# A decoder trunk on one core: retention heads projected with 512 moving columns, reciprocal roots as powers on GpSimd, a shorter last stage

## The chip, the cores and the metric

The kernel runs on one core of a Trainium2 chip. The metric is the device time of one launch in microseconds (us). The engines are named as in the profile: PE is TensorE's matmul side and PEld its weight loads, DVE is VectorE, ACT is ScalarE, POOL is GpSimd, SP is SyncE, which issues most of the DMAs.

## The reference

A residual stream x of 1024 tokens by 1024 channels goes through two layers and a final RMS norm. All is float32. A layer, cut to what matters here:

```python
mod = c_act @ w_ada[layer] + b_ada[layer]
shift, scale, gate = jnp.split(mod[:, None, :], 3, axis=-1)
h = rmsnorm(x, norm_g[layer]) * (1.0 + scale) + shift
proj = jnp.einsum('bld,de->ble', h, w_in[layer])      # one input projection, split into four branches
y_a = hgrn2_branch(...)       # 4 heads, vector decay
y_b = retention_branch(rq, rk, rv, rg, ret_onorm_g[layer])
y_c = ssd_branch(...)         # selective state space, 2 groups
y_d = gla_branch(...)         # 4 heads, vector decay
y = jnp.concatenate([y_a, y_b, y_c, y_d], axis=-1)
x = x + gate * jnp.einsum('ble,ed->bld', y, w_out[layer])
```

The retention branch has four heads of 128 channels: query and key are rotated by position (`[t1*cos - t2*sin, t1*sin + t2*cos]`, halves of 64), a chunked scalar-decay attention follows, then a group RMS norm per head and a SiLU gate. At the end comes `rmsnorm(x, final_g)`.

## The kernel before

**Arithmetic.** The input projection and the output projection are made from operands split in two parts of a rounded float32 type (`fp32r`). A weight tile `raw` is loaded (two buffers), ACT rounds it to `whi` (L408), DVE forms the rest `wlo` (L409), with four buffers for each. The normed input, feature-major, exists as `hh` and `hl` for all tokens. A product is three matmuls: hh*whi, hh*wlo, hl*whi.

**Projections.** There are two forms. `proj_f` (L423 to L425) makes 128 features by 512 tokens, with the weights stationary and 512 moving columns. `proj_t` (L470, L472, L473) makes a unit of 256 features token-major: for each k of eight, and each of eight token tiles, the input tile is stationary and 256 weight columns move. Its eight results lie two to a PSUM bank, four banks of the `pp` tag, all in use until the unit ends. Its weights come as four raw tiles, each with two k. A retention head has two such units: query with key (`rqk`), then value with gate (`rvg`).

**Retention.** `ret_qk` evacuates query and key by a copy on ACT (L842), four multiplications of 128x128 on DVE for each of query and key (L846 to L849), and two sums on POOL (L850, L851), for two token tiles at a time. `vg_proj` evacuates the value on DVE (L740) and the gate with SiLU on ACT (L741). `ret_mix` transposes query and key (L862), makes the scores (L875, L877) and calls `scan` (L664 to L680), which calls the head norm (L544, L548) and brings the result feature-major (L527, L535, L536) for the output projection.

**Roots.** `rsqrt_of` computes (s*scale + eps)^-0.5 on DVE from a bit trick and three Newton steps: L266, L271, L272, then three times L275, L276, L277, twelve tiny instructions one after another. It serves the norm of the input, every head norm, the state-space norm and the final norm.

**Order.** The order of TensorE's instructions is written out by hand. A mixer is a generator that yields how many ns its next product has to wait for others; the function `fill` then takes that much work from the deque `ready`, which holds projections and output projections. `drain` runs `ready` until a given unit has ended. A wrong estimate makes TensorE wait, since its queue is in order. Output projections (`add_out`) take two feature tiles at a time: weights loaded, multiplied by the gate on POOL (L1113), split, then 16 units of six matmuls (L1124) and an addition onto x on DVE (L1129). A unit yields after every third matmul.

In a layer the mixers come in this order: the four hgrn heads, the four gla heads, the two state-space groups, the four retention heads. Retention head 0 is projected while the second state-space group runs (its lines here are L1067, L1085, L1103), head h+1 while head h is mixed. The output projection of the last two feature tiles (6, 7) goes by token tiles, and each tile is normed as it is done: `next_norm` in the first layer, `final_after` in the second.

**The final norm.** For token tiles 0 to 6: squares on ACT (L355), a root on DVE, the tile times the gain on POOL (L1164, 128x1024), the scale on ACT (L1165), the DMA (L1168). The last tile goes in halves: two sums of squares (L1175), a root, two DVE instructions (L1185), two DMAs (L1186).

**The start.** x is loaded, its squares summed on ACT (L355), two roots for four token tiles each, the scaling (L373), transposes (L383). The shift and scale of the first layer are sums over `w_ada` on DVE (L302, L304), whose results `gs` (L320) allow the first `hh` (L400) and the first projections (L423).

Of the kernel before, what the change touches and what calls it, by code (L numbers as in the profile page):

```python
# [11 lines left out]
F32 = mybir.dt.float32  # L12
# [9 lines left out]
P = 128  # L22
# [11 lines left out]
# Columns of the combined input projection.  # L34
# [6 lines left out]
# Feature-major units (128 columns) and token-major units (256 columns).  # L41
# [33 lines left out]
# Per-partition columns, packed: name -> (offset, width).  # L75
# [20 lines left out]
# Rows that are broadcast over partitions.  # L96
# [16 lines left out]
# Constants that depend on shapes alone.  # L113
# [53 lines left out]
def hybrid_trunk(ctx, nc, tc, t_in, out, gamma_c):  # L167
# [94 lines left out]

    def rsqrt_of(ss, n, scale, eps):
        """(ss * scale + eps) ** -0.5, elementwise on [128, n]."""
        t = sm_t("rt", n, w=8)
        vec.tensor_scalar(t, ss, scale, eps, MUL, ADD)  # L266
        return rsqrt(t, n)

    def rsqrt(t, n):
        y = sm_t("ry", n, w=8)  # L270
        vec.tensor_scalar(y.bitcast(I32), t.bitcast(I32), 1, None, ALU.arith_shift_right)  # L271
        vec.tensor_scalar(y.bitcast(I32), y.bitcast(I32), -1, RSQRT_SEED, MUL, ADD)  # L272
        w = sm_t("rw", n, w=8)
        for _ in range(3):
            vec.tensor_tensor(w, y, y, MUL)  # L275
            vec.scalar_tensor_tensor(w, w, -0.5, t, MUL, MUL)  # L276
            vec.scalar_tensor_tensor(y, w, 1.5, y, ADD, MUL)  # L277
        return y
# [10 lines left out]
    def ada_sum(l, c0, n, out_):  # L289
        """Sum over k-tiles of w_ada[k, c0 : c0 + n] * silu(c)[k], per partition."""  # L290
# [32 lines left out]
    def set_gate(l, acc):  # L323
        """The gate on every partition."""
# [9 lines left out]
    # Lower bounds of the forget gates (the first layer's is zero).  # L334
# [28 lines left out]
    def over_rms(ms, ss, engs=(gp,)):  # L363
        """Token tiles over their rms; the last one is where the gate comes later."""
# [11 lines left out]
    def columns(xr):  # L376
        """Tiles xr of 512 tokens, feature-major, for each k."""
# [11 lines left out]
    def modulated(l, half, xr=None, xT=None):  # L389
        """The modulated norm of 512 tokens, feature-major, as the parts hh, hl; a step for each k."""  # L390
# [36 lines left out]
    def proj_f(l, name, evac):  # L427
        """Feature-major: evac(half, ps) takes 512 tokens of a unit's 128 features."""
# [27 lines left out]
    def proj_t(l, name, evac):  # L456
        """Token-major: evac(j, ps) takes token tiles 2j and 2j+1 as ps[128, 2, 256]."""
# [19 lines left out]

    def proj_t_wide(l, name, evac, extra):
# [982 lines left out]
```

## Time and profile before

| | |
|---|---|
| median of 3 runs | 2113.49 us (2113.32 to 2113.72) |
| span of the profiled execution | 2112.7 us |
| PE busy | 2047.3 us, 97% |
| DVE busy | 1318.1 us, 62% |
| ACT busy | 732.0 us, 35% |
| POOL busy | 389.0 us, 18% |
| mean granted TensorE clock | 0.991 |

The profile gives one time for its own execution, the span from the first instruction to the last. The median of the timed runs lies 0.8 us above it. In a row of a timeline stand the start, the duration, the engine, the line, the operation, output and inputs with their shapes, and in brackets how long the engine had been idle and what released it. In a group row stand the count, the busy time, the mean in ns and the idle time before. Durations of matmuls overlap: what a matmul costs is the distance between two starts.

### The profile page before, as it was taken

Reading aid. Unit: us, or ns where it says so; the run is one execution under the profiler, and the core shown is the slowest. Engines: PE = TensorE matmul, PEld = TensorE weight load, DVE = VectorE, ACT = ScalarE, POOL = GpSimd, SP = SyncE. Lnnn points to the kernel's source line nnn. Section 1 sums busy time; section 2 is a strip of 40 time slices with the busy share of each in tenths; the row PEclk is TensorE's granted clock in tenths of the full one; section 3 lists DMA queues with packets and bytes.
Section 4 is the critical chain, followed back from the end, with each engine's and each line's share of the span. In section 5 each row is a group of like instructions: output and inputs, shape, how many; then the busy total and the mean of one; then the engine's idle time right before and its main releaser. Section 6 shows DMA issues by size and latency. Waiting matters only on the chain.

```text
span 2112.7 us, 43480 instructions
## 1 busy us (share of the span) xinstructions
PE 2047.3 (97%) x18052; PEld 1835.8 (87%) x18052; DVE 1318.1 (62%) x3206; ACT 732.0 (35%) x1642; POOL 389.0 (18%) x493
## 2 busy tenths in 40 slices
PE   4999999999999999999999999999999999999996
PEld 3898888899888899999878888878988889999994
DVE  7657845847638576555676574575665676755568
ACT  6432224432333422222263232344233352222223
POOL 3100000000035253112120010000101535401133
PEclk8999999999999999999999999999999999999998
DMA  8233321110111111111122111111111111111111
GB/s 278 83 106 100 94 74 36 32 41 32 41 40 36 41 45 31 51 36 40 37 63 87 56 37 41 36 37 36 37 37 43 36 36 48 39 39 37 41 51 80
DMA packets 67542, 115.75 MB, mean 55 GB/s; under 512 B 9584, under 2 KB 19984, under 8 KB 67344
## 3 DMA queue, kind: packets, MB, share of 16 engines
q1 hardware_dynamic: 67056, 112.24, 16.5%
q8 instruction: 142, 2.33, 0.4%
q10 hardware_dynamic: 288, 0.73, 0.1%
q14 instruction: 56, 0.46, 0.1%
HBM read 108.75 MB, written 4.19 MB: 53 GB/s over the span
## 4 chain that ended last, share of the span: by engine, by line
PE 83%; DVE 11%; ACT 4%; issue 1%; DMA 1%; SPq 0%; DVEq 0%; ACTq 0%
PE pp L1124 14%; PE pp L470 11%; PE pp L472 11%; PE pp L473 11%; PE pp L423 6%; PE pp L425 6%; PE pp L424 6%; PE ms L670 2%; PE sc L587 1%; PE sc L527 1%; DVE b L615 1%; DVE xs L1129 1%; PE po L664 1%; PE sc L664 1%; PE sc L674 1%
## 5 line engine op out<-in xcount | busy, mean ns | idle before, releaser
L470 PE MATMUL pp<-whi,hh 128*128 128x256 f32 x2176 | 628.9, 289 | 0.7 <-ACT b L953 0.7
L472 PE MATMUL pp<-wlo,hh 128*128 128x256 f32 x2176 | 611.5, 281 | 0.0
L473 PE MATMUL pp<-whi,hl 128*128 128x256 f32 x2176 | 611.1, 281 | 0.0
L470 PEld LDWEIGHTS pp<-whi,hh 128*128 128x128 f32 x2176 | 410.3, 189 | 4.4 <-ACT b L953 1.6
L472 PEld LDWEIGHTS pp<-wlo,hh 128*128 128x128 f32 x2176 | 410.5, 189 | 0.8
L473 PEld LDWEIGHTS pp<-whi,hl 128*128 128x128 f32 x2176 | 410.1, 188 | 0.0
L408 ACT CAST whi<-raw 128x512 fp32r<-128x512 f32 x280 | 174.0, 625 | 600.5 <-PE pp L473 302.1
L409 DVE TENSOR_TENSOR wlo<-raw,whi 128x512 fp32r<-128x512 f32 x276 | 207.9, 755 | 250.2 <-ACT whi L408 243.2
L1113 POOL TENSOR_TENSOR raw<-raw,gate_b 128x512 f32<-128x512 f32 x64 | 82.8, 1295 | 1146.4 <-DMA raw<-in_w_out 895.3
L423 PE MATMUL pp<-hh,whi 128*128 128x512 f32 x640 | 272.1, 425 | 12.0 <-ACT hh L400 11.3
L425 PE MATMUL pp<-hl,whi 128*128 128x512 f32 x640 | 254.6, 398 | 1.3 <-DVE hl L401 1.3
L424 PE MATMUL pp<-hh,wlo 128*128 128x512 f32 x640 | 253.7, 396 | 0.0
L1129 DVE TENSOR_TENSOR xs<-xs,pp 128x512 f32<-128x512 f32 x256 | 173.7, 683 | 53.3 <-PE pp L1124 50.9
L1124 PE MATMUL pp<-whi,yh 128*128 128x512 f32 x448 | 189.0, 422 | 0.0
L1124 PE MATMUL pp<-whi,yl 128*128 128x512 f32 x448 | 175.4, 392 | 0.0
L1124 PE MATMUL pp<-wlo,yh 128*128 128x512 f32 x448 | 175.4, 392 | 0.0
L423 PEld LDWEIGHTS pp<-hh,whi 128*128 128x128 f32 x640 | 121.5, 190 | 36.5 <-ACT hh L400 12.6
L425 PEld LDWEIGHTS pp<-hl,whi 128*128 128x128 f32 x640 | 120.8, 189 | 33.2 <-DVE hl L401 4.4
L424 PEld LDWEIGHTS pp<-hh,wlo 128*128 128x128 f32 x640 | 121.6, 190 | 20.9 <-DVE wlo L409 0.2
L1124 PEld LDWEIGHTS pp<-whi,yh 128*128 128x128 f32 x448 | 84.4, 188 | 20.5 <-issue 3.0
L304 DVE SCALAR_TENSOR_TENSOR b<-wa,c_act,b 128x512 f32<-128x512 f32 x84 | 70.2, 835 | 51.2 <-DMA wa<-in_w_ada 50.3
L1124 PEld LDWEIGHTS pp<-whi,yl 128*128 128x128 f32 x448 | 84.1, 188 | 18.8
(242 smaller groups left out, 3195.5 us busy)
## 6 DMA issues: line engine op xcount, KB each, us to landing
raw<-in_wt SPq DMA_DIRECT2D x136, 256.0 KB, 3.0
wa<-in_w_ada SPq DMA_DIRECT2D x96, 256.0 KB, 2.8
raw<-in_wf SPq DMA_DIRECT2D x80, 256.0 KB, 2.6
raw<-in_w_out SPq DMA_DIRECT2D x64, 256.0 KB, 2.5
xs<-in_x SPq DMA_DIRECT2D x8, 512.0 KB, 7.4
out<-b SPq DMA_DIRECT2D x7, 512.0 KB, 2.6
b<-in_wt SPq DMA_DIRECT2D x4, 384.0 KB, 4.8
b<-in_rows SPq DMA_DIRECT2D x4, 256.0 KB, 3.9
```

Source lines behind the costliest of these rows:

```text
L304: vec.scalar_tensor_tensor(acc, w, c_act[:, k : k + 1], acc, MUL, ADD)
L408: act.copy(hi, raw)
L409: eng.tensor_tensor(lo, raw, hi.bitcast(F32), SUB)
L423: pe.matmul(ps, hi[:, j : j + P], hh[half][:, k, :], start=(k == 0), stop=False)
L424: pe.matmul(ps, lo[:, j : j + P], hh[half][:, k, :], start=False, stop=False)
L425: pe.matmul(ps, hi[:, j : j + P], hl[half][:, k, :], start=False, stop=(k == KT - 1))
L470: pe.matmul(o, hhi, hi[:, j : j + 256], start=(k == 0 and m % 2 == 0), stop=False, skip_group_check=True)
L472: pe.matmul(o, hhi, lo[:, j : j + 256], start=False, stop=False, skip_group_check=True)
L473: pe.matmul(o, hlo, hi[:, j : j + 256], start=False, stop=(k == KT - 1), skip_group_check=True)
L1113: gp.tensor_tensor(raw, raw, gate_b[:, nh * 512 : (nh + 1) * 512], MUL)
L1124: pe.matmul(ps, a[:, o : o + P], b, start=(n == 0), stop=(n == 3 * len(kts) - 1))
L1129: vec.tensor_tensor(xv, xv, ps, ADD)
```

## The change

1. **Projection.** A new function `proj_pair` projects the query, key, value and gate of a retention head together, 512 columns. It goes through the tokens in two halves of four tiles; in each half through eight k. For each half and k it loads a raw tile of 512 columns by two DMAs of 128x256, so each weight is loaded and split twice. Each of the four `pp` banks holds one token tile.
2. **Rotation.** Query is copied out by ACT, key and value by DVE, the gate by ACT with SiLU, each 128x128. After the fourth tile of a half, query and key are each multiplied by the sines into a temporary and by the cosines in place, on DVE, 128x512; POOL makes the difference and the sum, 128x256.
3. **Roots.** `rsqrt_of` becomes two POOL instructions: multiply and add, then a power with a constant tile of -0.5.
4. **Order.** An output unit yields once, after its addition. The gate, shift and scale sums that hgrn heads 0 to 2 accumulate are finished in the next head. Before the retention heads, output tiles 10 and 11 are queued and 5 us of filler is run; the next head's projection is put in front of `ready`; output tiles 4 and 5 are queued at head 1 instead of after head 2; 5 us of filler follows each head. `ret_mix` yields 1500 after each half's transposes instead of 1200 after both.
5. **The final norm.** The squares are scaled by 1024^-0.5. A token tile's scaling by root and gain is one DVE instruction, made when the next tile's squares have been issued. The last tile is multiplied by the gain in halves, then scaled in halves, on DVE and ACT.

The diff, cut to its core:

```diff
+    mhalf = cst.tile([P, 8], F32, name="mhalf")
+    gp.memset(mhalf, -0.5)
     def rsqrt_of(ss, n, scale, eps):
         t = sm_t("rt", n, w=8)
-        vec.tensor_scalar(t, ss, scale, eps, MUL, ADD)
-        return rsqrt(t, n)
+        gp.tensor_scalar(t, ss, scale, eps, MUL, ADD)
+        r = sm_t("ry", n, w=8)
+        gp.tensor_tensor(r, t, mhalf[:, 0:n], ALU.pow)
+        return r
...
+    def proj_pair(l, names, evac):
+        src = t_in["wt"][l]
+        for half in range(2):
+            pss = [ps_proj() for _ in range(4)]
+            for k in range(KT):
+                raw = raw_t(512)
+                for i, name in enumerate(names):
+                    nc.sync.dma_start(raw[:, i * 256 : i * 256 + 256],
+                                      src[T_UNITS[name]][:, k * 256 : k * 256 + 256])
+                hi, lo = split(raw, 512)
+                for m in range(4):
+                    hhi = hh[half][:, k, m * P : m * P + P]
+                    hlo = hl[half][:, k, m * P : m * P + P]
+                    pe.matmul(pss[m], hhi, hi, start=(k == 0), stop=False)
+                    pe.matmul(pss[m], hhi, lo, start=False, stop=False)
+                    pe.matmul(pss[m], hlo, hi, start=False, stop=(k == KT - 1))
+                    if k == KT - 1:
+                        evac(4 * half + m, pss[m])
+                    yield 690
...
-    def ret_qk(l, h, tables, u):
+    def ret_proj(l, h, tables, u):
...
+        def ev(m, ps):
+            if m == 0:
+                u["q"], u["k"] = vg_tiles()
+                u["v"], u["g"] = vg_tiles()
+            act.copy(u["q"][:, m, :], ps[:, 0:128])
+            vec.tensor_copy(u["k"][:, m, :], ps[:, 128:256])
+            vec.tensor_copy(u["v"][:, m, :], ps[:, 256:384])
+            act.activation(u["g"][:, m, :], ps[:, 384:512], AF.Silu)
+            if m % 4 == 3:
+                ms_ = slice(m - 3, m + 1)
+                for qk in ("q", "k"):
+                    x = u[qk][:, ms_, :].rearrange("p m (e d) -> p m e d", e=2)
+                    t = mid_t().rearrange("p (m e d) -> p m e d", m=4, e=2)
+                    for dst, by in ((t, tables[1]), (x, tables[0])):
+                        vec.tensor_tensor(dst, x, bc(by[:, ms_, :].unsqueeze(2), [P, 4, 2, 64]), MUL)
+                    gp.tensor_tensor(x[:, :, 0, :], x[:, :, 0, :], t[:, :, 1, :], SUB)
+                    gp.tensor_tensor(x[:, :, 1, :], x[:, :, 1, :], t[:, :, 0, :], ADD)
+        yield from proj_pair(l, (("rqk", h), ("rvg", h)), ev)
...
     def out_unit(l, kts, w, m, nh):
-            if n < 3 * len(kts):
-                yield 640
-        yield 640
+        yield 640 * len(kts)
...
+    def final_after(m, nh):
+        s = slice(nh * 512, nh * 512 + 512)
+        if m < NT - 1:
+            if nh:
+                ss = sm_t("ss", 1, w=8)
+                scaled_squares(xs[:, m, :], ss)
+                if m:
+                    final_scale(m - 1, fin["r"])
+                fin["r"] = final_rms(ss, EPS)
+            return
+        if nh == 0:
+            fin["y"] = big_t()
+        y = fin["y"]
+        ss = sm_t("ss", 1, w=8)
+        scaled_squares(xs[:, m, s], ss)
+        vec.tensor_tensor(y[:, s], xs[:, m, s], final_gain()[:, s], MUL)
...
+        final_scale(m - 1, fin["r"])
+        r = final_rms(ss, fin["t"])
+        vec.tensor_scalar(y[:, 0:512], y[:, 0:512], r, None, MUL)
+        act.activation(y[:, 512:D], y[:, 512:D], AF.Copy, scale=r)
...
+        add_out(l, (10, 11))
+        fill(5000)
         for h in range(3):
             nu = {}
-            if h == 0:
-                add_out(l, (10, 11))
-            add(ret_qk(l, h + 1, tables, nu))
-            p = add(vg_proj(l, ("rvg", h + 1), nu))
+            p = ret_proj(l, h + 1, tables, nu)
+            ready.appendleft(p)
             run(ret_mix(l, h, u))
+            if h == 1:
+                add_out(l, (4, 5))
             drain(p)
+            fill(5000)
             u = nu
-        add_out(l, (4, 5))
```

Three places in the engines' order follow; names end in running numbers.

DVE in layer 0, where a retention head's query and key unit ends and its value and gate unit runs. Before (L849 is the last rotation multiplication, `wlo` the low weight parts, L740 the copies of the value):

```order
L849 TENSOR_TENSOR b_1537_10540<-b_1526_10455,b_1253_8556 128x128
L409 TENSOR_TENSOR wlo_10716<-raw_10713,whi_10715 128x512
L409 TENSOR_TENSOR wlo_10811<-raw_10808,whi_10810 128x512
L409 TENSOR_TENSOR wlo_10892<-raw_10889,whi_10891 128x512
L409 TENSOR_TENSOR wlo_10999<-raw_10996,whi_10998 128x512
L740 COPY b_1554_10749<-pp_10547 128x256
L740 COPY b_1554_10749<-pp_10548 128x256
L740 COPY b_1554_10749<-pp_10549 128x256
L740 COPY b_1554_10749<-pp_10550 128x256
```

The changed kernel's DVE at a head's half boundary (L403 makes the low parts, L855 and L856 copy key and value, L864 rotates):

```order
L403 TENSOR_TENSOR wlo_9246<-raw_9242,whi_9245 128x512
L855 COPY b_1426_9200<-pp_8951 128x128
L856 COPY b_1427_9201<-pp_8951 128x128
L855 COPY b_1426_9200<-pp_8952 128x128
L856 COPY b_1427_9201<-pp_8952 128x128
L855 COPY b_1426_9200<-pp_8953 128x128
L856 COPY b_1427_9201<-pp_8953 128x128
L855 COPY b_1426_9200<-pp_8954 128x128
L856 COPY b_1427_9201<-pp_8954 128x128
L864 TENSOR_TENSOR b_1429_9228<-b_1425_9199,b_1219_8293 128x512
L864 TENSOR_TENSOR b_1430_9233<-b_1426_9200,b_1219_8293 128x512
L864 TENSOR_TENSOR b_1425_9199<-b_1425_9199,b_1219_8293 128x512
```

One more L864 follows, then the low parts of the second half's second weight tile. Only the low part of its first tile stands ahead of the copies.

DVE at the very end. Before:

```order
L277 SCALAR_TENSOR_TENSOR ry_23613<-rw_23616,ry_23613 128x1
L275 TENSOR_TENSOR rw_23616<-ry_23613 128x1
L276 SCALAR_TENSOR_TENSOR rw_23616<-rw_23616,rt_23599 128x1
L277 SCALAR_TENSOR_TENSOR ry_23613<-rw_23616,ry_23613 128x1
L1185 SCALAR_TENSOR_TENSOR b_3457_23626<-xs,ry_23613,b_3391_23328 128x512 x2
```

After (L1142 is the addition onto x, L1178 the scaling of a whole tile, L1203 the last tile times the gain, L1210 its scaling):

```order
L1142 TENSOR_TENSOR xs<-xs,pp_21613 128x512
L1178 SCALAR_TENSOR_TENSOR b_3529_21624<-xs,ry_21602,b_3489_21471 128x1024
L1142 TENSOR_TENSOR xs<-xs,pp_21630 128x512
L1203 TENSOR_TENSOR b_3532_21638<-xs,b_3489_21471 128x512
L1142 TENSOR_TENSOR xs<-xs,pp_21645 128x512
L1178 SCALAR_TENSOR_TENSOR b_3539_21657<-xs,ry_21627,b_3489_21471 128x1024
L1203 TENSOR_TENSOR b_3532_21638<-xs,b_3489_21471 128x512
L1210 TENSOR_SCALAR b_3532_21638<-b_3532_21638,ry_21660 128x512
```

No root is left on DVE; a scaling of 1024 columns stands between the last addition and the last half tile.

POOL where the first output projection of layer 0 begins, after the change (L1128 multiplies output weights by the gate, L269 and L271 are a root):

```order
L1128 TENSOR_TENSOR raw_2517<-raw_2517,gate_b 128x512
L269 TENSOR_SCALAR rt_2187<-ss_2178 128x4
L271 TENSOR_TENSOR ry_2189<-rt_2187,mhalf 128x4
L1128 TENSOR_TENSOR raw_2524<-raw_2524,gate_b 128x512
L269 TENSOR_SCALAR rt_2278<-ss_2269 128x4
L271 TENSOR_TENSOR ry_2280<-rt_2278,mhalf 128x4
```

Before, the gate multiplications stood there without anything between them. Now a root waits for the weights' DMA ahead of it.

More of the change, by code (lines that the diff above doesn't have):

```diff
@@ L261, in hybrid_trunk @@
         gp.memset(ATs[i], 0.0)
+    mhalf = cst.tile([P, 8], F32, name="mhalf")
+    gp.memset(mhalf, -0.5)
     def rsqrt_of(ss, n, scale, eps):
         t = sm_t("rt", n, w=8)
-        vec.tensor_scalar(t, ss, scale, eps, MUL, ADD)
-        return rsqrt(t, n)
[L269 to L278, printed above, removed]
+        gp.tensor_scalar(t, ss, scale, eps, MUL, ADD)
+        r = sm_t("ry", n, w=8)
+        gp.tensor_tensor(r, t, mhalf[:, 0:n], ALU.pow)
+        return r
     def bc(ap, shape):
@@ L863, in ret_mix @@
                 act.copy(dst[:, half * 512 : half * 512 + 512], ps)
+            yield 1500
         o, _ = CST["rke"]
@@ L1156, in final_gain @@
         return fin["fg"]
-    def final_tiles(ms, engs):
-        fg = final_gain()
-        r = rsqrt_of(squares(ms), len(ms), 1.0 / D, EPS)
-        for i, (m, eng) in enumerate(zip(ms, engs)):
-            yo = big_t()
-            if eng is act:
-                gp.tensor_tensor(yo, xs[:, m, :], fg, MUL)
-                act.activation(yo, yo, AF.Copy, scale=r[:, i : i + 1])
-            else:
-                eng.scalar_tensor_tensor(yo, xs[:, m, :], r[:, i : i + 1], fg, MUL, MUL)
-            nc.sync.dma_start(out[m * P : (m + 1) * P, :], yo)
@@ L1170, in final_half, with scaled_squares, final_scale, final_rms @@
-    def final_half(m, nh):
-        s = slice(nh * 512, nh * 512 + 512)
+    def scaled_squares(xv, ss):
+        junk = mid.tile([P, 1024], BF16, tag="b2", name=nm("junk"))[:, : xv.shape[1]]
+        act.activation(junk, xv, AF.Square, scale=D ** -0.5, accum_out=ss)
+    def final_scale(m, r):
+        yo = big_t()
+        vec.scalar_tensor_tensor(yo, xs[:, m, :], r, final_gain(), MUL, MUL)
+        nc.sync.dma_start(out[m * P : (m + 1) * P, :], yo)
+    def final_rms(t, more):
+        r = sm_t("ry", 1, w=8)
+        gp.tensor_scalar(r, t, more, None, ADD)
+        gp.tensor_tensor(r, r, mhalf[:, 0:1], ALU.pow)
+        return r
@@ L1173, in final_half @@
+    def final_after(m, nh):
+        s = slice(nh * 512, nh * 512 + 512)
+        if m < NT - 1:
[9 more added lines that the diff above has]
+        y = fin["y"]
         ss = sm_t("ss", 1, w=8)
-        junk = mid.tile([P, 512], BF16, tag="b2", name=nm("junk"))
@@ L1175, in final_half @@
-        act.activation(junk, xs[:, m, s], AF.Square, accum_out=ss)
+        scaled_squares(xs[:, m, s], ss)
+        vec.tensor_tensor(y[:, s], xs[:, m, s], final_gain()[:, s], MUL)
         if nh == 0:
             fin["t"] = sm_t("rt", 1, w=8)
-            vec.tensor_scalar(fin["t"], ss, 1.0 / D, EPS, MUL, ADD)
+            gp.tensor_scalar(fin["t"], ss, EPS, None, ADD)
             return
-        vec.scalar_tensor_tensor(fin["t"], ss, 1.0 / D, fin["t"], MUL, ADD)
-        r = rsqrt(fin["t"], 1)
@@ L1182, in final_half @@
-        yo, fg = big_t(), final_gain()
-        for i in range(2):
-            s = slice(i * 512, i * 512 + 512)
-            vec.scalar_tensor_tensor(yo[:, s], xs[:, m, s], r, fg[:, s], MUL, MUL)
-            (nc.sync, nc.scalar)[i].dma_start(out[m * P : (m + 1) * P, s], yo[:, s])
-    def final_after(m, nh):
-        if m == NT - 1:
-            final_half(m, nh)
-        elif m < 4:
-            if nh:
-                final_tiles([m], [(act,act)[m % 2]])
-        elif nh:
-            final_tiles([m], [act])
+        final_scale(m - 1, fin["r"])
@@ L1199, in hybrid_trunk @@
+        r = final_rms(ss, fin["t"])
+        vec.tensor_scalar(y[:, 0:512], y[:, 0:512], r, None, MUL)
+        act.activation(y[:, 512:D], y[:, 512:D], AF.Copy, scale=r)
+        nc.sync.dma_start(out[m * P : (m + 1) * P, 0:512], y[:, 0:512])
+        nc.scalar.dma_start(out[m * P : (m + 1) * P, 512:D], y[:, 512:D])
     start = tc.manual_schedule(engines={nc.sync.engine})
@@ L1290, in hybrid_trunk @@
         next(steps)
+        sums_of = {}
         for h in range(4):
@@ L1305, in hybrid_trunk @@
                 run(hgrn_scores(l, h, u))
+            if h - 1 in sums_of:
+                (lambda a: set_gate(l, a), lambda a: set_shift(l + 1, columns_of(a)),
+                 lambda a: set_scale(l + 1, columns_of(a)))[h - 1](sums_of[h - 1])
             run(hgrn_scan(l, h, u))
@@ L1356, in hybrid_trunk @@
                 tables = []
-                add(ret_qk(l, 0, tables, nu))
-                p = add(vg_proj(l, ("rvg", 0), nu))
+                p = add(ret_proj(l, 0, tables, nu))
             run(ssd_mix(l, g, u, st, lambda: more_x(nu) if g == 0 else None))
```

26 lines of the change are left out of this document (1 added, 25 removed).

## The prediction

> **What bounds the kernel now.** I began with the engines' shares, then the chain of work that ended last.
>
> ```profile
> PE 2047.3 (97%) x18052; PEld 1835.8 (87%) x18052; DVE 1318.1 (62%) x3206; ACT 732.0 (35%) x1642; POOL 389.0 (18%) x493
> PE 83%; DVE 11%; ACT 4%; issue 1%; DMA 1%; SPq 0%; DVEq 0%; ACTq 0%
> ```
>
> TensorE is busy for 97% of the 2112.7 us, so time can be won in two ways only: by spacing its matmuls more closely, or by taking away the few places where it stands still. The table of what TensorE waited for lists these:
>
> ```profile
> PE pp L383 <- DVE b L373: 14.0, 1, 14.0
> PE pp L423 <- ACT hh L400: 11.3, 4, 8.7
> PE po L1067 <- DVE s L1085: 3.1, 4, 1.1
> PE pp L1124 <- DVE xs L1129: 2.9, 3, 1.9
> PE sc L527 <- DVE b L1103: 2.4, 2, 1.2
> ```
>
> The first two are the start, the fourth is the last stage, and the third and fifth are the state-space mixer, during which retention head 0 is projected. Nothing in retention itself is on the list: its projections are steady filler, and there the pitch decides.
>
> **The pitch (gain).** Timeline of TensorE: a stretch of the retention-style projection (256 columns), one of the output projection and one of the feature-major projection (both 512 columns); start, duration, line.
>
> ```profile
> 599.84 0.28 PE L470 MATMUL pp<-whi,hh 128*128 128x256 f32 x1
> 611.90 0.28 PE L470 MATMUL pp<-whi,hh 128*128 128x256 f32 x1
> ...
> 1029.99 0.39 PE L1124 MATMUL pp<-whi,yh 128*128 128x512 f32 x1
> 1034.52 0.39 PE L1124 MATMUL pp<-whi,yl 128*128 128x512 f32 x1
> ...
> 44.08 0.40 PE L423 MATMUL pp<-hh,whi 128*128 128x512 f32 x1
> 44.78 0.39 PE L423 MATMUL pp<-hh,whi 128*128 128x512 f32 x1
> ```
>
> Between the first pair lie 102 matmuls: 12.06 / 102 = 118.2 ns each. Between the second pair lie 20: 4.53 / 20 = 226.5 ns. Between the third lie 3: 233 ns. One matmul of 512 columns thus replaces two of 256 (236.5 ns) and saves 10.0 ns by L1124 or 3 ns by L423. The change takes 8 heads x 192 = 1536 matmuls away. I take L1124, because like the new code it gives the same stationary tile to its first two matmuls and the other to the third: 1536 x 10.0 = **-15**, with -5 as the other bound. The Trainium skill ("TensorE: Matmul & The Clock Gate", "Wait — 56ns, not 53.3ns?") has a warm pitch of columns / 2.4 GHz plus about 2.5 ns. By it merging would save 2.5 ns each, 3.8 us in all, and the sum would end 11 us higher. The trace does not agree in absolute terms, since 118.2 ns and 226.5 ns stand against 109 and 216; what the merged form pays per instruction, no run shows yet.
>
> **The end (gain).** Last rows of TensorE, VectorE and the queues, with two rows of groups that price what is new there:
>
> ```profile
> 2096.12 0.40 PE L1124 MATMUL pp<-whi,y 128*128 128x512 f32 x1
> 2097.71 0.68 DVE L1129 TENSOR_TENSOR xs<-xs,pp 128x512 f32<-128x512 f32 x1
> 2099.77 2.34 POOL L1164 TENSOR_TENSOR b<-xs,b 128x1024 f32<-128x1024 f32 x1 [2.58 <-DVE rw L275]
> 2099.79 2.33 DVE L276 SCALAR_TENSOR_TENSOR rw<-rw,rt 128x1 f32<-128x1 f32 x1
> 2107.88 0.16 DVE L276 SCALAR_TENSOR_TENSOR rw<-rw,rt 128x1 f32<-128x1 f32 x1
> 2108.27 1.41 DVE L1185 SCALAR_TENSOR_TENSOR b<-xs,ry,b 128x512 f32<-128x512 f32 x2
> 2109.72 0.36 ACTq L1186 DMA_DIRECT2D out<-b  x1
> ...
> L956 DVE SCALAR_TENSOR_TENSOR b<-b,cols,b 128x1021 f32<-128x1021 f32 x16 | 21.0, 1310 | 0.0
> L302 DVE TENSOR_SCALAR b<-wa,c_act 128x512 f32<-128x512 f32 x12 | 6.8, 565 | 0.2
> ```
>
> From the last matmul's end (2096.52) to the span's end it is 16.2 us. VectorE is why: a step of a reciprocal root on one column lasts 0.16 us (2107.88), but 2.33 us (2099.79) while GpSimd multiplies 128x1024 (L1164), which it does seven times. In the changed kernel neither exists. What is left after the last matmul: the addition 0.68; on VectorE the scaling of tile 6 (priced by L956, 1.31) and half a tile times the gain (about 0.7), in whose shadow ACT's squares and GpSimd's two instructions run; one half-tile scaling 0.57; and 3.0 from the last VectorE result to the end (2112.7 - 2109.68). With 0.3 for handovers that is 6.6, so **-9.6**. The power itself has no row. Nearest are a GpSimd instruction on one column (below) and the chain that it replaces, 2.4 us in the start rows; at 2.4 it would stick out by 1.4 here, so -8 is the bound.
>
> ```profile
> L1452 POOL MEMSET const-float32-1.0<- 128x1 f32 x1 | 0.1, 108 | 0.0
> ```
>
> I take 0.2 each, nearer the one-column row since four columns are no more work.
>
> Before that end, VectorE will need 2 x 0.68 + 1.31 = 2.67 per token tile and TensorE 12 x 0.2265 = 2.72, so the wait on L1129 (2.9) should go: **-3** (0 to -4).
>
> **The start and the mixer (gain).** VectorE, start and duration:
>
> ```profile
> 10.81 0.17 DVE L266 TENSOR_SCALAR rt<-ss 128x4 f32<-128x4 f32 x1 [4.13 <-ACT junk L355]
> 13.20 2.74 DVE L373 TENSOR_SCALAR b<-xs,ry 128x1024 f32<-128x1024 f32 x4
> 16.25 0.16 DVE L266 TENSOR_SCALAR rt<-ss 128x4 f32<-128x4 f32 x1
> 18.50 8.57 DVE L304 SCALAR_TENSOR_TENSOR b<-wa,c_act,b 128x512 f32<-128x512 f32 x7
> 34.13 0.15 DVE L320 TENSOR_TENSOR gs<-sc,cols 128x2 f32<-128x2 f32 x1
> ```
>
> The two roots hold VectorE for 2.4 and 2.25 us. The first stands ahead of the first transposes, the second ahead of the conditioning sums, whose result (34.13) the first projections await. Sums that wait for their DMAs keep part of it: **-3** (0 to -5). In the mixer both waits, 3.1 and 2.4, arise where rotations or a stretched root stand ahead on VectorE; the rotations now come at the ends of halves: **-4** (0 to -5.5). Elsewhere some 65 more roots leave VectorE, off the path: worth nothing. On GpSimd they stand between gate multiplies (1.3 us each), and behind a root its norm waits, then the transposes to feature-major; 2.4 us or more of filler is asked for before these, so I cost that at nothing, up to 5 if weights come late.
>
> **What it costs.** Groups, and two DMA rows (size, landing time):
>
> ```profile
> L409 DVE TENSOR_TENSOR wlo<-raw,whi 128x512 fp32r<-128x512 f32 x276 | 207.9, 755 | 250.2 <-ACT whi L408 243.2 <-PE po L674 6.8
> L408 ACT CAST whi<-raw 128x512 fp32r<-128x512 f32 x280 | 174.0, 625 | 600.5 <-PE pp L473 302.1 <-PE pp L1124 97.6 <-issue 82.6
> L846 DVE TENSOR_TENSOR b<-b,b 128x128 f32<-128x128 f32 x64 | 18.4, 287 | 15.8 <-ACT b L842 15.8
> L847 DVE TENSOR_TENSOR b<-b,b 128x128 f32<-128x128 f32 x64 | 30.8, 481 | 0.0
> L877 DVE TENSOR_TENSOR at<-sc,cs 128x512 f32<-128x512 f32 x16 | 11.0, 690 | 11.5 <-PE sc L875 11.5
> L678 DVE COPY st<-ms 128x128 f32<-128x128 f32 x24 | 7.0, 290 | 35.7 <-PE ms L670 35.7
> raw<-in_wt SPq DMA_DIRECT2D x136, 256.0 KB, 3.0
> b<-in_wt SPq DMA_DIRECT2D x2, 256.0 KB, 4.3
> ```
>
> Loading each weight tile twice adds 64 casts (40 us of ACT) and 64 subtractions (48 us of VectorE), both hidden in total, since VectorE loses 70 roots of about 2.25 us. Their timing matters. At a head's half boundary four PSUM tiles end 0.68 apart. VectorE's order then holds the last tile's two copies (2 x 0.29), four multiplications (4 x 0.69) and only then the low part of the second weight tile (0.69): with 0.2 of handover, ready 4.2 us after the half's last matmul. TensorE has tile one ready, 12 x 0.2265 = 2.72, plus one matmul on the second's high part: it needs the low part at 2.95, so it waits 1.3. If GpSimd's rotations stretch the last two of these as they do L847 against L846 (481 / 287 = 1.7), each grows by 0.5 and it waits 2.3. Over seven boundaries (8 heads, one counted next) 9 to 16; **+12**, nothing if scan matmuls fall there.
>
> At the first head of each layer the value and gate tiles are asked for at the end of half 0, together with query and key, while the mixer still reads its own tiles; the evacuation then waits for a buffer. That can cost up to a half's evacuation on each layer, 0 to 5 each; **+4** in all. Output-projection filler is used earlier, so less is left for the last head: its transposes and the weights of the last tiles (landing 3.0 + cast 0.6 + subtraction 0.8) have less cover, 0 to 6 per layer; **+6**.
>
> **Sum.** -15 - 9.6 - 3 - 3 - 4 + 12 + 4 + 6 = -12.6 on the profiled span of 2112.7, so 2100; the median of the runs, 2113.5, lies 0.8 above that span. Forecast: 2101.
>
> **Rivals.** *Starved projection (slower).* A weight tile now lasts TensorE 2.72 us instead of 16 x 0.355 = 5.67. Its buffer goes round in two issues on SP (0.7), landing, cast 0.63, subtraction 0.75 and 0.2; with two buffers the pace is half of that. At a landing of 3.0 it is 2.64, just enough; the limit is 3.16. The change asks for 1 KB pieces, as did the row with 4.3 us, and then the pace is 3.29: 0.57 short on each of 128 tiles, 73 us if nothing covered it. A head has other matmuls too, so that only stretches of pure projection suffer; with a third of the tiles, +24: **2125**. Against it: that 4.3 was taken with other transfers in flight, and the DMA engines are mostly idle in this part.
>
> *No new waits.* If filler and scans cover every boundary, the +22 fall away but for a few: **2084**. For it: no wait of retention is on today's list. Against it: the order of VectorE above.
>
> *The merged matmul runs like L423.* Then 10 less is won: **2111 to 2115**, within what a measurement tells from no change (0.2%, 4 us). For it: in both the moving tensor has 512 columns and stationary tiles alternate. This is also where the 2.5 ns of the Trainium skill would lead.
>
> **Chances.** Forecast 0.42 (its own range 2093 to 2110), starved 0.24, no new waits 0.18, pitch like L423 0.16. The range takes in half of each outer case: 2086 to 2121. Faster: the forecast but for 0.03, all of the second rival, a little of the third: 0.58. Slower: starved but for a little, 0.23; the rest, 0.19, no change.
>
> **What would show it.** L486 to L488 at 226 ns between starts (233 means the third rival); after the last matmul less than 7 us; no tiny instruction of 2 us on VectorE at the end; L383's wait near 12 instead of 14.0; new waits of 1 to 2.5 us on L487 for the low part (L403) at the half boundaries, seven times. Waits on L487 at many tiles inside a half mean starvation. A GpSimd power above 1 us, or norms that wait behind a gate multiply, would make the forecast wrong in a way that I priced at nothing.

## The result: 2138.4 us, slower by 1.1%

The changed kernel took 2138.39 us (median of 4 runs, 2133.60 to 2139.06) against 2113.60 for the kernel before (2113.32 to 2114.41). The ratio is 1.0112, with a 95% interval of 1.0097 to 1.0126. I had forecast 2101 and a range that ended at 2121. One execution of e3_256 below (3434 us) and one of e9_pad (7057 us, the profiled one) were far slower than their like, so these two runs' times are medians of the other executions, and e9_pad has no trace to read.

The profiled execution after the change spans 2136.0 us. Shares of the engines:

```profile
PE 2053.1 (96%) x16516; PEld 1772.5 (83%) x16516; DVE 1215.6 (57%) x2341; ACT 762.6 (36%) x1736; POOL 439.9 (21%) x564
```

VectorE lost 102 us of work and GpSimd gained 51. TensorE has 1536 matmuls fewer, yet is busy 6 us longer: it ran part of the time at a lower clock. Of its waits, as total, times and longest:

```profile
PE pp L486 <- ACT b L857: 12.1, 6, 5.3
PE sc L542 <- DVE b L563: 9.4, 4, 3.6
PE pp L487 <- DVE wlo L403: 6.2, 4, 1.7
PE pp L1139 <- DVE wlo L403: 3.8, 2, 1.9
...
PE pp L1139 <- ACT y L550: 1.9, 1, 1.9
PE pp L1139 <- DVE y L551: 1.2, 1, 1.2
```

The first is the SiLU of the gate at a half boundary, the second the head norm of a last head, the third the low weight part behind the rotation; the other three are the weights and the last transposed tiles of the output projection. All lie in the retention stage. In the list before, the first and the third had no like. The head norm of the last head had one, which I had passed over: of the three waits in this line, the longest stands at 2074.59, in layer 1's last retention head.

```profile
PE sc L527 <- DVE b L548: 2.5, 3, 1.2
```

**Where the time went.** I cut both executions at the same instructions: the first feature-major matmul (L423, now L417), the last of it in layer 0, the first in layer 1, the last in layer 1, and the last matmul. Between the second and the third, and after the fourth, lie the end of the state-space mixer, retention and the last output projection. TensorE's timelines, of the kernel before:

```profile
37.63 0.79 PE L423 MATMUL pp<-hh,whi 128*128 128x512 f32 x1 [8.72 <-ACT hh L400]
709.95 0.39 PE L423 MATMUL pp<-hh,whi 128*128 128x512 f32 x1
1068.55 0.48 PE L423 MATMUL pp<-hh,whi 128*128 128x512 f32 x1
1732.74 0.39 PE L423 MATMUL pp<-hh,whi 128*128 128x512 f32 x1
```

and of the changed kernel:

```profile
32.37 0.79 PE L417 MATMUL pp<-hh,whi 128*128 128x512 f32 x1 [4.13 <-ACT hh L394]
705.48 0.39 PE L417 MATMUL pp<-hh,whi 128*128 128x512 f32 x1
1087.77 0.48 PE L417 MATMUL pp<-hh,whi 128*128 128x512 f32 x1
1750.18 0.39 PE L417 MATMUL pp<-hh,whi 128*128 128x512 f32 x1
2126.30 0.39 PE L1139 MATMUL pp<-whi,y 128*128 128x512 f32 x1
```

| part | before | after | change |
|---|---|---|---|
| start | 37.6 | 32.4 | -5.3 |
| layer 0 to the retention stage | 672.3 | 673.1 | +0.8 |
| retention stage, layer 0 | 358.6 | 382.3 | +23.7 |
| layer 1 to the retention stage | 664.2 | 662.4 | -1.8 |
| retention stage, layer 1 | 363.4 | 376.1 | +12.7 |
| after the last matmul's start | 16.6 | 9.7 | -6.9 |

So the start and the end together gave about what they were to give, and the two retention stages, which I had summed to about nothing, lost 36.

**Place 1: the first head's half boundary.** Timeline of layer 0, where retention head 0 is projected during the mixer:

```profile
795.66 1.12 POOL L1049 TENSOR_TENSOR s<-b,rbdsk 128x128 f32<-128x128 f32 x2 [0.42 <-DVE b L1103]
796.41 0.79 ACT L857 ACTIVATE b<-pp 128x128 f32<-128x128 f32 x4 [4.58 <-POOL s L1049]
796.74 0.80 PE L486 MATMUL pp<-whi,hh 128*128 128x512 f32 x1 [5.27 <-ACT b L857]
```

The four SiLUs wait for a buffer that the mixer's GpSimd instructions still read; the PSUM banks are not free before them, and TensorE waits 5.3 us. What follows is seen in stretches of 2 us (length, PE busy, then the granted clock):

```profile
796.00:798.00 2.00, 1.26 (x3) 0.50 0.01 0
...
802.00:804.00 2.00, 2.00 (x10) 0.93 0.00 0
```

From 796 to 802 the clock is half. By an estimate from these figures (half of 6 us) that costs another 3 us, and I had not priced it. Both layers show it alike.

**Place 2: the other half boundaries.** Head 1 in layer 0:

```profile
864.59 2.49 DVE L864 TENSOR_TENSOR b<-b,b 128x512 f32<-128x512 f32 x4
867.00 2.36 DVE L403 TENSOR_TENSOR wlo<-raw,whi 128x512 fp32r<-128x512 f32 x2
868.27 0.50 PE L487 MATMUL pp<-wlo,hh 128*128 128x512 f32 x1 [1.37 <-DVE wlo L403]
```

Two low parts last 2.36 us instead of 1.4, while GpSimd rotates. This is the wait that I had worked out at 1.3 to 2.3 us. It took 1.4 to 1.7, but came four times, not seven.

**Place 3: the last head.** Layer 0, timeline, and the clock in a stretch of 3 us behind it:

```profile
1051.95 1.13 DVE L563 SCALAR_TENSOR_TENSOR b<-po,ry,b 128x128 f32<-128x128 f32 x4 [3.33 <-POOL ry L271]
1052.45 1.16 PE L542 MATMUL sc<-cs,b 128*128 128x128 f32 x4 [3.60 <-DVE b L563]
...
1053.00:1056.00 3.00, 3.00 (x14) 0.50 0.00 0
```

Here the chain of the head norm (the root on GpSimd, then L563) stands open, since no output projection is left to put over it.

### The profile page after: what moved, and what is told of

It reads as the page before. It is cut to its first block, busy times and chain, and to the rows that moved or that the text cites. A ratio compares the mean times of both kernels' runs of the same rounds, so it can differ in the third digit from the quotient of the medians.

```text
span 2136.0 us, 40215 instructions
## 1 busy us (share of the span) xinstructions
PE 2053.1 (96%) x16516; PEld 1772.5 (83%) x16516; DVE 1215.6 (57%) x2341; ACT 762.6 (36%) x1736; POOL 439.9 (21%) x564
## 4 chain that ended last, share of the span: by engine, by line
PE 81%; DVE 9%; ACT 5%; issue 2%; DMA 2%; POOL 1%; SPq 0%; POOLq 0%; ACTq 0%; DVEq 0%
PE pp L1139 14%; PE pp L417 6%; PE pp L419 6%; PE pp L418 6%; PE pp L464 6%; PE pp L466 6%; PE pp L467 6%; PE pp L486 5%; PE pp L487 5%; PE pp L488 5%; PE ms L685 2%; PE sc L602 2%; DVE wlo L403 1%; DMA wa<-in_w_ada 1%; PE po L1082 1%
## 5 line engine op out<-in xcount | busy, mean ns | idle before, releaser
L403 DVE TENSOR_TENSOR wlo<-raw,whi 128x512 fp32r<-128x512 f32 x340 | 258.2, 762 | 316.5 <-ACT whi L402 309.3
L464 PE MATMUL pp<-whi,hh 128*128 128x256 f32 x1152 | 335.4, 291 | 0.7 <-ACT b L968 0.7
L466 PE MATMUL pp<-wlo,hh 128*128 128x256 f32 x1152 | 325.7, 283 | 0.0
L467 PE MATMUL pp<-whi,hl 128*128 128x256 f32 x1152 | 325.6, 283 | 0.0
L417 PE MATMUL pp<-hh,whi 128*128 128x512 f32 x640 | 270.6, 423 | 7.4 <-ACT hh L394 6.7
L486 PE MATMUL pp<-whi,hh 128*128 128x512 f32 x512 | 214.2, 418 | 12.3 <-ACT b L857 12.1
L464 PEld LDWEIGHTS pp<-whi,hh 128*128 128x128 f32 x1152 | 220.4, 191 | 3.9 <-ACT b L968 1.5
L466 PEld LDWEIGHTS pp<-wlo,hh 128*128 128x128 f32 x1152 | 220.7, 192 | 0.3
L467 PEld LDWEIGHTS pp<-whi,hl 128*128 128x128 f32 x1152 | 220.5, 191 | 0.0
L1142 DVE TENSOR_TENSOR xs<-xs,pp 128x512 f32<-128x512 f32 x256 | 172.1, 683 | 64.9 <-PE pp L1139 63.3
L487 PE MATMUL pp<-wlo,hh 128*128 128x512 f32 x512 | 201.8, 394 | 6.2 <-DVE wlo L403 6.2
L488 PE MATMUL pp<-whi,hl 128*128 128x512 f32 x512 | 201.9, 394 | 0.0
L1128 POOL TENSOR_TENSOR raw<-raw,gate_b 128x512 f32<-128x512 f32 x64 | 84.0, 1312 | 547.8 <-DMA raw<-in_w_out 332.8
L417 PEld LDWEIGHTS pp<-hh,whi 128*128 128x128 f32 x640 | 121.1, 189 | 30.1 <-ACT hh L394 8.6
```

The source lines that it names most:

```text
L403: eng.tensor_tensor(lo, raw, hi.bitcast(F32), SUB)
L417: pe.matmul(ps, hi[:, j : j + P], hh[half][:, k, :], start=(k == 0), stop=False)
L464: pe.matmul(o, hhi, hi[:, j : j + 256], start=(k == 0 and m % 2 == 0), stop=False, skip_group_check=True)
L466: pe.matmul(o, hhi, lo[:, j : j + 256], start=False, stop=False, skip_group_check=True)
L467: pe.matmul(o, hlo, hi[:, j : j + 256], start=False, stop=(k == KT - 1), skip_group_check=True)
L486: pe.matmul(pss[m], hhi, hi, start=(k == 0), stop=False)
```

## The experiments

The retention stage of each kernel, cut as above, stands in the table; times are medians, with the median of the kernel before in the same session.

| run | time | before | ratio (95%) | stage, layer 0 | stage, layer 1 |
|---|---|---|---|---|---|
| changed kernel | 2138.4 | 2113.6 | 1.0112 (1.0097 to 1.0126) | 382.3 | 376.1 |
| e1_roots_final | 2103.2 | 2114.0 | 0.9949 (0.9932 to 0.9965) | 362.8 | 361.3 |
| e2_proj | 2165.3 | 2114.0 | 1.0241 (1.0226 to 1.0256) | 384.9 | 388.8 |
| e3_256 | 2133.9 | 2114.0 | 1.0098 (1.0081 to 1.0115) | 380.2 | 374.4 |
| e4_order | 2132.2 | 2114.0 | 1.0085 (1.0070 to 1.0100) | 376.4 | 374.7 |
| e5_256_order | 2103.2 | 2114.9 | 0.9947 (0.9932 to 0.9961) | 361.2 | 360.0 |
| e6_nofill | 2129.6 | 2114.9 | 1.0067 (1.0050 to 1.0084) | 378.8 | 372.0 |
| e7_start_final | 2098.9 | 2114.9 | 0.9925 (0.9910 to 0.9940) | 361.0 | 358.8 |
| e8_start_final_rot | 2095.9 | 2114.9 | 0.9912 (0.9898 to 0.9927) | 360.1 | 357.8 |
| e9_pad | 2117.0 | 2115.2 | 1.0009 (1.0000 to 1.0019) | no trace | no trace |
| e10_best_pad | 2086.5 | 2115.2 | 0.9870 (0.9853 to 0.9886) | 357.0 | 352.2 |
| e11_best_off | 2091.7 | 2115.2 | 0.9890 (0.9876 to 0.9905) | 358.0 | 355.9 |
| e12_best_pad96 | 2090.5 | 2114.3 | 0.9887 (0.9870 to 0.9903) | 357.0 | 354.4 |

### e1_roots_final: the parts that were to gain, alone

```diff
 (the kernel before)
-        vec.tensor_scalar(t, ss, scale, eps, MUL, ADD)
-        return rsqrt(t, n)
+        gp.tensor_scalar(t, ss, scale, eps, MUL, ADD)
+        r = sm_t("ry", n, w=8)
+        gp.tensor_tensor(r, t, mhalf[:, 0:n], ALU.pow)
+        return r
 (and the final norm of the change)
```

> The kernel before with only the roots on GpSimd and the new final norm. Theory (the loss lies in the retention stage: waits of the merged projection, and a last head without filler): these two parts keep what the ledger of the changed kernel shows for them, 5 at the start, 7 behind the last matmul and the 3 of the last stage's waits, so about 2099 (2096 to 2103). Rival (roots on GpSimd make norms late everywhere): above 2110, with new waits on L527 spread over the layers.

2103.2, at the edge of what the theory gave. The roots and the final norm gain 11 us. The rival falls: no norm waits are spread over the layers. A new wait, though, costs 3.7 in two places:

```profile
PE pp L1129 <- DVE wlo L414: 3.7, 2, 1.9
```

### e2_proj: the merged projection and the rotation, alone

The diff is that of the change for `proj_pair` and `ret_proj`; both stand in the old order as one unit at the end of `ready`.

> The kernel before with only the merged projection and the new rotation, in the old order. Theory: the wait of 5 us at the first head's half boundary and the 1.4 to 1.7 us at others appear in each layer, and a slower clock behind them, against a closer pitch worth 10 in all: 2112 to 2122. Rival (the new order of filler causes the loss): none of the long waits, 2100 to 2105. Rival (weights come too slowly): above 2130.

2165.3. Only the rival of weights that come too slowly had a time in this region (above 2130), and its reason is not the one. Nor is any of the named waits: the first head of each layer waits 1.3 us, not 5, and no half boundary waits for a low part. The wait list begins with a place that I had passed over (L883 is the transposition of query and key, L872 GpSimd's part of the rotation):

```profile
PE sc L883 <- POOL b L872: 36.8, 8, 6.2
PE po L883 <- POOL b L872: 2.9, 8, 0.7
```

Eight heads wait 5 us each. Before, the query and key unit came first and the value and gate unit behind it, 64 x 0.355 = 23 us for the rotation to end in. In the merged form query and key are finished with the last matmul, and the transposes come next. Weights that come late are excluded: L493 (the matmul that needs the low part) is not on the list at all.

### e3_256 and e4_order: each of the two undone

```diff
 (e3: the changed kernel)
-        yield from proj_pair(l, (("rqk", h), ("rvg", h)), ev)
+        yield from proj_t(l, ("rqk", h), ev_qk)     # rotates after each fourth tile
+        yield from proj_t(l, ("rvg", h), ev_vg)
 (e4: the changed kernel)
-        yield 640 * len(kts)
+        yield 640                                   # and one after every third matmul
...
-        add_out(l, (10, 11))
-        fill(5000)
...
-            ready.appendleft(p)
-            fill(5000)
```

In e4 the output tiles 10, 11 and 4, 5 are also queued again where they were. Of the order, two things stay as changed in e4: `ret_mix` yields 1500 after each half, and the conditioning sums are finished a head later.

> The changed kernel with its retention heads projected in two units of 256 columns again (key copied on VectorE, rotation four tiles at once, order and all else as changed). Theory: the 5.3 us wait of each first head and the half-boundary waits go, the closer pitch too, the last head's waits stay: 2138 - 2 x (5.3 + 3.5 + 3) - some slow clock 6 + pitch 10 = about 2119 (2112 to 2126). Rival (order alone): 2138 + 10 = 2148 or no less than 2138.

> The changed kernel with the old order in the retention stage (output units yield twice, output tiles 10, 11 and 4, 5 queued where they were, no extra filler, projection at the end of the list). Theory: the last head's waits (1.9 + 3.6 + 1.3 + 1.9 in layer 0, 1.9 + 3.6 + 0.9 + 1.2 in layer 1, and slow clock behind them, some 23 in all) go, the first head's stay: 2112 to 2120. Rival (order alone): near 2100. Rival (projection alone): 2135 or more.

2133.9 and 2132.2: both miss the forecast, by 8 and 12 us. Undoing one part gives back 4 or 6 of the 25 us. Two rivals come nearer, within 3 to 4 us of their bounds: that the order alone is the cause (e3), and that the projection alone is (e4). Both cannot be true, yet either edit by itself keeps nearly all of the loss. The wait lists say why. In e3 the list has L542 at 9.4 us again, word for word as the changed kernel; in e4 it begins:

```profile
PE sc L877 <- POOL b L866: 22.0, 8, 4.0
PE po L877 <- POOL b L866: 4.8, 8, 0.7
```

With the new order, the last heads lack filler, whatever form the projection has. With the old order, the transposes wait for the rotation. They wait less than in e2 (37 + 3 us); that the longer yields of `ret_mix` are the reason is likely, but no run shows it. The list of e4 also tells where the first head's 5.3 us come from: there the same matmul (L486 on L857) waits 1.3 at most, although the projection is merged. Up to that place of layer 0 the two programs differ in one thing only, that an output unit yields twice in e4 and once in the changed kernel, which moves the half boundary against the mixer.

From this came a new theory: the two edits belong together. The merged form needs cover at the end of each head, the new order takes it from the output projections (a stock that is fixed per layer), and the last head then has none.

### e5_256_order: both undone

The two diffs above at once.

> The changed kernel with both undone at once: projections in two units of 256 columns and the old order; roots, final norm, the new rotation and the later conditioning sums stay. Undoing one of the two moved the time by 3 and 6 us only. Theory (the two belong together: the merged form brings query and key to the very end of a head, where the old order has nothing to cover the rotation, and the new order covers it with filler that the last head then lacks): undone together they give back some 35, so 2098 to 2105. Rival (another part costs the time, the rotation or the roots): 2112 or more.

2103.2, as the new theory had it, and as e1 without the new rotation. One undone gives 4, the other 6, both together 35. The loss lies in the pair, and its parts do not add up: against e5 the new order alone costs 31 us (e3), the merged form alone 29 (e4), and both together 35.

### e6_nofill: the filler given back to the last head

```diff
             drain(p)
-            fill(5000)
```

> The changed kernel without the 5 us of filler behind each of the first three retention heads. Theory: the waits move from the last head to the transposes. L877 waits for GpSimd's rotation 3 to 5 us at heads 1 to 3 of both layers, 15 to 25 in all, while L542's wait of 3.6 and the waits on the last output weights go: 2128 to 2142. Rival (the last head does not lack filler): L542 keeps its 3.6 and the time rises above 2145.

2129.6, inside the theory's range, and faster than the changed kernel. L542's total falls from 9.4 to 3.8. The wait for the low part of the output weights (3.8) is gone too, those on the last transposed tiles (1.9 and 1.2) stay. The waits on the rotation are smaller than I said, 6.5 instead of 15 to 25, for a reason that no run tells. The three fills behind heads cost 9 us more than they cover.

```profile
PE sc L542 <- DVE b L563: 3.8, 4, 1.3
PE po L877 <- POOL b L866: 3.7, 4, 1.2
PE sc L877 <- POOL b L866: 2.8, 4, 0.8
```

### e7_start_final and e8_start_final_rot: a better kernel

```diff
 (e7: the kernel before, with the final norm of the change)
-    def over_rms(ms, ss, engs=(gp,)):
-        r = rsqrt_of(ss, len(ms), 1.0 / D, EPS)
+    def over_rms(ms, ss, engs=(gp,), root=rsqrt_of):
+        r = root(ss, len(ms), 1.0 / D, EPS)     # the two calls at the start pass the GpSimd root
 (e8: as e7, and in ret_qk's evacuation)
+            if j % 2 == 0:
+                return
+            ...                                 # the rotation of four tiles at once
```

> The kernel before with the final norm of the change and with GpSimd roots at the start alone; all other roots stay on VectorE. By the ledger of the run with all roots, 5 come at the start, 7 behind the last matmul, 3 to 4 before it, and the 2.7 that its first layer lost at the end of retention and the 0.5 per head are not paid: 2096 to 2100. Rival (those losses have another cause than roots in GpSimd's queue): 2103 as with all roots.

> The kernel before with the final norm, GpSimd roots at the start alone and the rotation of four tiles at once (projections of 256 columns, old order). Theory: the waits of the state-space mixer on rotations (3.1 + 2.4 in all) mostly go: 2091 to 2096. Rival (longer multiplications on VectorE delay others): no better than without the rotation, 2097 or more.

2098.9 and 2095.9, both times as the theory gave them. Roots on GpSimd help at the start, where they stand on the path; at the end they came together with the shorter last stage, and no run parts the two. In between they cost 4 to 5 us: the run with all roots waits 3.7 for output weights, e7 only 0.4. The rotation of four tiles gives 3. Of the two mixer waits that it was to end, one falls from e7 to e8 (on the tiles `s`, 3.7 to 1.3), the other does not (on the mixer's result, 2.3 and 2.8).

### e9 to e12: where the tiles stand

Comparing the runs showed something that no edit had meant: the pitch of matmuls that the change does not touch is another one in every kernel with the constant tile `mhalf`. This tile of 32 bytes per partition moves all weight and work tiles behind it (not `hh` and `hl`, which stand ahead of it). The same 185 steps of a 256-column projection in layer 0, first and last row, before the change and after it:

```profile
598.31 0.39 PE L470 MATMUL pp<-whi,hh 128*128 128x256 f32 x1 [0.18 <-ACT b L953]
620.30 0.28 PE L473 MATMUL pp<-whi,hl 128*128 128x256 f32 x1
```

```profile
595.18 0.39 PE L464 MATMUL pp<-whi,hh 128*128 128x256 f32 x1 [0.18 <-ACT b L968]
617.47 0.28 PE L467 MATMUL pp<-whi,hl 128*128 128x256 f32 x1
```

21.99 us against 22.29, or 118.9 ns against 120.5.

```diff
 (e9: the kernel before)       + mhalf = cst.tile([P, 8], F32, name="mhalf"), filled, not used
 (e10: e8)                     - cst.tile([P, 8], ...)   + cst.tile([P, 16], ...)
 (e12: e8)                     - cst.tile([P, 8], ...)   + cst.tile([P, 24], ...)
 (e11: e8)                     - hi = wp.tile([P, SL], ...)[:, :n]
                               + hi = wp.tile([P, SL + 16], ...)[:, o : o + n]   # o = 8 in proj_t, else 0
```

> The kernel before with nothing but the constant tile of 32 bytes per partition allocated, unused: it moves every weight and work tile behind it by 32 bytes, to a multiple of 64. Theory (in all runs with this tile the pitch of 256 columns is 119.8 ns against 118.3 without it, and the feature-major projection's 230 against 233, and the place of the tiles is the reason): 6528 x 1.5 = +9.8 and 1920 x 3.2 = -6.1, so +3 to +4: 2116 to 2119, with these two pitches. Rival (roots on GpSimd or the new final norm change the pitch): 2113 to 2115 and the pitches of before.

> The kernel with the final norm, GpSimd roots at the start and the new rotation, its constant tile widened from 32 to 64 bytes, so that the tiles behind it stand again where they stood before the change. Theory (place of the tiles): pitches 118.3 and 233, 3 to 4 faster than without, 2091 to 2094. Rival: 2095 to 2097.

> The same kernel with the narrow constant tile (tiles at multiples of 64 bytes), but the high weight part begins 32 bytes further on where it moves through TensorE with 256 columns. Theory (place of the moving operand decides the 256-column pitch, place of the stationary one the feature-major pitch): the two matmuls of three that move the high part go at 118.3, the third stays at 119.8, the feature-major form stays at 230: 6 faster, 2088 to 2092. Rival (the place of another tile decides): 2095 to 2097 and 119.8 for all three.

> The kernel with the final norm, GpSimd roots at the start and the new rotation, its constant tile 96 bytes wide, so that the weight and work tiles behind it stand at an odd multiple of 64 bytes (with 32 bytes they stood at an even one, with 64 bytes 32 further). Theory that only the place within 64 bytes counts: the pitches of the 32-byte tile, 119.8 and 230, and 2094 to 2097. Rival (a finer or wider pattern counts): another pitch of 256 columns than 119.8 or 116.9, and a time outside 2094 to 2097.

An unused tile alone makes the kernel before slower by 1.8 us, less than the 3 to 4 forecast and at the edge of what can be told from nothing; whether its pitches changed is not known. Widening the tile from 32 to 64 bytes makes the better kernel 9.4 us faster, against 3 to 4 forecast: 2086.5, the best of all. The same 185 steps there, and in e12:

```profile
591.45 0.39 PE L480 MATMUL pp<-whi,hh 128*128 128x256 f32 x1 [0.18 <-ACT b L962]
613.14 0.28 PE L483 MATMUL pp<-whi,hl 128*128 128x256 f32 x1
```

```profile
592.81 0.38 PE L480 MATMUL pp<-whi,hh 128*128 128x256 f32 x1 [0.18 <-ACT b L962]
614.71 0.28 PE L483 MATMUL pp<-whi,hl 128*128 128x256 f32 x1
```

| kernel | first `whi` tile, bytes modulo 128 | 256 columns, ns | feature-major, ns |
|---|---|---|---|
| before | 96 | 118.9 | 233 |
| changed, e1, e3 to e8 | 0 | 120.5 | 229 |
| e10_best_pad | 32 | 117.3 | 233 |
| e12_best_pad96 | 64 | 118.4 | 233 |

(The addresses are those of the built programs; the 256-column pitch is from the stretch above, for the second row that of the changed kernel; the feature-major one is the mean over all its matmuls without those that wait.) That the place within 64 bytes decides is refuted: e12 stands at a multiple of 64, as the changed kernel does, and has other pitches. Moving the high part alone (e11) gave 4 us, less than half of e10. The time is the one forecast, but not for its reason: from its start to the next, the two matmuls that move the high part took 118.8 ns on average and the third, with the low part left in place, 116.6, the reverse of what I expected. So the place of the tiles changes the pitch by up to 3%, and which operand does it stays open.

## Why the prediction was wrong

- **The pitch** was right in size: the merged matmuls take 229 ns on average, 1536 x (2 x 118.3 - 229) = 12 us against 15 forecast. But the reason for choosing L1124's pitch, the stationary tile used twice, is wrong. In e2, which has no constant tile, the same code runs at 233 ns, like L423, so that merging by itself saves 3.6 ns each (2 x 118.3 - 233). The difference goes with the place of the tiles: 1536 x 4 = 6 of the 12 us came with 32 bytes that another part of the change added. That the size came out is luck.
- **The start** gained 5.3 against 3, but not where I looked: the wait for the first transposes (L383) went from 14.0 to 13.6 only, the one of the first projections (L423) from 11.3 to 6.7. **The mixer's** two waits (3.1 and 2.4) are gone, but the first head's 5.3 stands in the same stretch; the wait on L1129 in **the last stage** (2.9) is gone as forecast.
- **The end:** -6.9 against -9.6. Rows of VectorE and GpSimd after the last matmul's start (2126.30):

```profile
2127.02 0.68 DVE L1142 TENSOR_TENSOR xs<-xs,pp 128x512 f32<-128x512 f32 x1
...
2128.34 0.68 DVE L1142 TENSOR_TENSOR xs<-xs,pp 128x512 f32<-128x512 f32 x1
2128.94 1.28 DVE L1178 SCALAR_TENSOR_TENSOR b<-xs,ry,b 128x1024 f32<-128x1024 f32 x1
2130.01 0.87 POOL L1183 TENSOR_SCALAR ry<-ss,rt 128x1 f32<-128x1 f32 x1 [1.19 <-ACT junk L1174]
2130.97 0.57 POOL L1184 TENSOR_TENSOR ry<-ry,mhalf 128x1 f32<-128x1 f32 x1
2131.57 0.49 DVE L1210 TENSOR_SCALAR b<-b,ry 128x512 f32<-128x512 f32 x1 [0.75 <-POOL ry L1184]
```

GpSimd's two instructions take 1.44 there, not 0.4; the first takes 0.87 beside VectorE's scaling L1178. The half tile waits 0.75 for them. That is the smaller part of the 2.7 that are missing: the last addition begins 1.65 after the end of the last matmul (2126.69), behind an addition and a product with the gain that I had not put there, and from the last VectorE result (2132.06) to the end it is 3.9, not 3.0.

- **The power** was mis-sized. Group rows:

```profile
L271 POOL TENSOR_TENSOR ry<-rt,mhalf 128x4 f32<-128x4 f32 x58 | 59.9, 1032 | 4.8
L1184 POOL TENSOR_TENSOR ry<-ry,mhalf 128x1 f32<-128x1 f32 x8 | 4.6, 569 | 0.7
```

"Four columns are no more work" is false: (1032 - 569) / 3 = 154 ns per column. A root of four columns takes 1.3 us on GpSimd, against 2.4 on VectorE. It is still a gain where it stands on the path (start: -5.3 against -3 forecast).

- **The half boundaries** (+12 forecast) cost 6.2 in waits: mechanism right, four boundaries instead of seven. Seven was a miscount, since the first heads of both layers were counted in the next term, which leaves six. At head 2 of each layer TensorE did not stand still.
- **"The evacuation then waits for a buffer ... +4 in all"**: this step failed in size. It is two waits of 5.3, and the clock behind each. In e2 and e4, in the old order, it is 1.3.
- **"Output-projection filler is used earlier, so less is left ... +6"** is the step that failed most. L542, the output weights and the last transposed tiles wait 16.3 us (9.4 + 3.8 + 1.9 + 1.2; before, 1.9 in the same places), and the clock falls behind the longest ones. I had asked what the filler is taken from, but not counted it. "Nothing in retention itself is on the list" was a misreading: the head norm's wait of 1.2 us in layer 1's last head, before, showed already how little cover was left there.
- **What I did not see at all** is why the filler was needed: that the merged form ends query and key at the end of a head (e2: 37 + 3 us). I had costed the edit to the order without asking what it covers.
- **The slow clock** was in no term. The two retention stages of each kernel, cut as above (length, time that TensorE is busy with its count of rows in brackets, granted clock, share of the DMA engines, GB/s), before and after:

```profile
709.95:1068.55 358.60, 355.57 (x2621) 1.00 0.12 38
1732.74:2096.12 363.38, 356.57 (x2607) 1.00 0.13 42
```

```profile
705.48:1087.77 382.29, 361.36 (x1853) 0.97 0.20 58
1750.18:2126.30 376.12, 356.84 (x1839) 0.98 0.22 66
```

TensorE stands still for 9.8 us before and 40.2 after: 30 of the 36 us. It is busy 6 us longer, although the closer pitch takes 12 away. An estimate from the clock's column, 382 x 0.03 + 376 x 0.02 = 19 us, accounts for about that much; part of it falls into the waits themselves and costs nothing more.
- **The starved projection**, my slower rival, gave the nearest time (2125) for a wrong reason: a tile of two 128 KB pieces lands in 2.5 us, the round is short enough, and no run shows a wait inside a half.

```profile
raw<-in_wt SPq DMA_DIRECT2D x256, 128.0 KB, 2.5
```

What stays open: the order was undone only as a whole, so which of its edits uses up the filler is not known, but for the three fills behind heads (9 us, e6). The shares of wait and clock are read from the traces; no run took away one of them alone.

## What to carry to other kernels

Where an order is written by hand, filler is a stock: before an edit that adds a wait is costed, count what is left of it at the last place that needs it, and ask of every edit to the order what it covers. When two products are merged, look at when each half of the result was ready before and who came next; the time that lay between was cover. And a wait on TensorE of about 2 us or more costs more than its length here, because the clock is lower for some microseconds behind it.

## What the runs showed of the hardware

- After a wait of 5.3 us the granted clock was 0.50 for 6 us. A shorter wait was enough too:

```profile
1029.99 0.50 PE L1139 MATMUL pp<-wlo,yh 128*128 128x512 f32 x1 [1.91 <-DVE wlo L403]
1031.91 0.63 PE L1139 MATMUL pp<-wlo,yh 128*128 128x512 f32 x1
...
1032.00:1035.00 3.00, 3.00 (x14) 0.60 0.29 98
```

The matmul begins after 1.9 us of waiting; two microseconds later its like lasts 0.63 instead of 0.39, and for 3 us the clock is 0.60. The Trainium skill ("TensorE: Matmul & The Clock Gate", Part 1) has the clock halve after an idle window of about 3.4 us. This trace agrees on the half, not on the length of the wait. In the kept traces, after the first 80 us, all 33 waits of TensorE of 1.87 us or more have a stretch of half clock within them or beginning at most 3.5 us behind them; of the 47 waits from 1.0 to 1.8 us two have one.
- Tiles moved by 32 bytes change the start-to-start pitch: 256 moving columns from 117.3 to 120.5 ns, the feature-major form from 229 to 233 ns, the merged form from 229 to 233 ns. On this kernel that is worth up to 9 us, nearly as much as the new roots and the final norm together (11).
- A power on GpSimd took 0.57 us for one column, 0.70 for two and 1.03 for four.
